# Six PSUM banks in turn, work given out ahead of read-outs, and wide tiles with their high weights first, in one layer of a hybrid decoder

## The chip, the cores and the metric

The kernel runs on one core of a Trainium2 chip. Its time is the device time of one execution in microseconds (us); lower is better. Names: PE is TensorE (PEld its weight loads), DVE is VectorE, ACT is ScalarE, POOL is GpSimd, SP is the queue that issues most DMAs.

## What is computed

One layer for a sequence of 256 positions and a width of 1024, in float32:

```
n = RMSNorm(x)
h = x + W_mix_out( g_conv * ConformerConv(n) + g_attn * DSA(n) )   # one input projection W_in of n
h = h + CrossAttn(RMSNorm(h), RMSNorm(mem))                        # 4 heads, 256 memory tokens
h = h + W2 relu(W1 RMSNorm(h))^2                                   # width 4096
out = RMSNorm(h)
```

ConformerConv gates a projection by a sigmoid, runs a causal depthwise convolution of 31 taps over the positions, takes a LayerNorm and a silu, and multiplies by a 1024 x 1024 matrix. DSA has 8 heads of 128, with a small index attention that chooses 64 keys for each query. All parameters are read once (92.21 MB from HBM with the inputs).

## The kernel before

**Activations stand feature by position**: a tile is 128 features x 256 positions, eight of them (`kt` 0 to 7) a tensor. Every float32 operand of a large product is split in two, a high part rounded to the matmul's format (`hi`) and the rest (`lo`), and a product is made of three: high weight by high activation, high by low, low by high. ACT makes `hi` of a weight by a copy and DVE makes `lo` by a subtraction, 1024 columns at a time; two such halves make a chunk of 1 MB that SP loads into one of three `raw` buffers. Up to six halves are held.

**The stream.** Chunks come in a fixed order, and so do the stages: xk (keys of the memory), conv (the convolution's input and gate, 4 of 8), qi and ki (index attention), conv (the other 4), gc (convolution gate), v, q and k in turn, ga (attention gate), ao (attention out), co (convolution out), mix (mix out), xq, xv and xo (cross attention), f1 and f2 in turn (feed forward; in the profile f and ff).

**A tile of 128 output features** is 8 steps `kt`. In a *narrow* tile (`mm3`) a step is three matmuls of 256 columns. In a *wide* one (`tile_b` with `wide`, L303) the high weight meets high and low activations side by side in one matmul of 512 columns, and the low weight the high activations in one of 256; the two halves of the PSUM bank are then added by `total` (L340): ACT copies the second half out, DVE adds the first. qi, q, k, ga, ao, xq and f are wide, conv, gc, co and mix narrow. Form b (`form_b`, L313) makes two such tiles of a chunk; each takes a PSUM bank from `ps_mm`, of which there are two. Four more banks (`ps_acc`) serve v, xv, xo, f2 and small products, two (`ps_aux`) the rest.

**What sets the order.** The program is written out by hand, engine by engine, with a running estimate of each engine's time (`Counted`: L89 is the line that issues every recorded instruction, so nearly all rows name it). After each tile `tick` (L247) resumes the `chains` (generators for heads, norms and the like), then gives DVE taps of the convolution from `fill` while its total is under PE's plus 1000 (ns), runs the read-outs' second halves that stand in `due`, and gives ACT one pair of tap products, which POOL adds into `added` by an accumulating DMA (42 of these). 148 taps are done on DVE (`acc`), the rest by those DMAs. ACT and DVE work off what they are given in that order.

**Around the middle.** When all taps are in, `layer_norm` normalises the convolution; it waits until the ga gate's sigmoid is done (`gates`), then takes silu on ACT and splits the result into `u2` on DVE (CAST and subtraction), which co needs. `gated` multiplies co's product by the gates, `residual` adds mix's product to `h_t` and splits it for xq. A cross head (`cross_head`) is a generator: scores, softmax, transposes, values.

Of the kernel before, what the change touches and what calls it, by code (L numbers as in the profile page):

```python
# [22 lines left out]
BEHIND = 1000  # L23
AHEAD = 1000
# [83 lines left out]
def block_kernel(ctx, tc, x, xt, mem, memt, wst, wki, vecs, convw, gout, out):  # L108
# [36 lines left out]

    class Pair:
# [99 lines left out]

    def tick():  # L247
# [4 lines left out]
        while later:  # L252
            later.pop(0)()
        if low_jobs and len(prepared) < READY and nturn[0] > 4:
            split_low()
        while (len(fill) > 1 or (fill and (len(done) > 5 or nused[0] < 5))) and dve.total < pe.total + (BEHIND if due else AHEAD):
            fill_one()
        while due:
            due.pop(0)()
        for g in groups:  # L260
            if g.ready() and scalar.total < pe.total + 1300:
                g.products()
                groups.remove(g)
                groups.append(g)
                break
        for g in halves:
            g.finish()
# [4 lines left out]
        dve.total = max(dve.total, pe.total - 2000)  # L272
        scalar.total = max(scalar.total, pe.total - 2000)
# [92 lines left out]
    def load_memory(q):  # L366
        for kt in ((0,), (2, 4), (6,), ())[q]:
            nc.sync.dma_start(mem_t[:, kt : kt + 2, :], memt[:, kt : kt + 2, :])

    load(4, load_memory)  # L370
# [21 lines left out]
    for j in range(9):  # L392
# [104 lines left out]
    def memory_parts():  # L497
# [4 lines left out]
        mem2.append(Pair("mem"))  # L502
        for kt in range(KT + 1):
            if kt < KT:
# [35 lines left out]
    class Half:  # L540
# [7 lines left out]
        def finish(self, now=False):  # L548
# [3 lines left out]
            self.open = False  # L552
            g = self.g
            both = acc[:, 4 * g : 4 * g + 4, :]
            dve.tensor_tensor(out=both, in0=both, in1=added[:, 4 * g : 4 * g + 4, :], op=ALU.add)
            pair = w2(f"usum{g}", F32, (P, 2, S))
# [162 lines left out]
    def layer_norm():  # L719
# [8 lines left out]
        for c, cs in enumerate(pairs):  # L728
# [3 lines left out]
            if c % 2 == 1:  # L732
                yield
# [524 lines left out]
```

## Time and profile before

| | us |
|---|---|
| median of 3 runs | 530.05 (529.81 to 530.83) |
| the profiled execution | 528.47 |
| its span, first to last instruction | 526.4 |
| PE busy / DVE / ACT / POOL | 507.4 / 400.9 / 322.3 / 44.6 |
| weights' lo on DVE, 161 | 195.2 |
| weights' hi on ACT, 161 | 168.1 |
| taps on DVE, 148 | 63.2 |

Where the stages lie, by the first matmul of each, in us from the span's start: conv 22.7, qi 45.9, ki 58.4, conv again to 90.2, gc 90.2, v 113.3, q and k 135.1, ga 190.7, ao 217.9, co 242.7, mix 268.2, xq 291.3, xv 305.3, xo 319.6, f 336.9. A row of a timeline gives start, length, engine, line, operation, what is written and read, the shape, how often in a row, and in brackets the engine's idle time before it and what ended it. Matmuls overlap their neighbours, so the pace of a stage is read from starts, not from lengths. A row of waits gives who waited for whom: us in total, times, longest.

### The profile page before, as it was taken

The page shows a single profiled execution, that of the slowest core. Times are in us where ns is not written, and L with a number is a line of the kernel's source. Part 1 is how long each engine was busy: PE and PEld are TensorE (multiplying, and loading weights), DVE is VectorE, ACT ScalarE, POOL GpSimd, SP SyncE. Part 2 cuts the span into 40 slices and gives each one's busy share as a digit, 9 for nine tenths or more (in the row PEclk, how much of TensorE's full clock was granted, in tenths as well). Part 3 has the DMA queues.
Part 4 walks back from the last instruction along what each step waited for, and adds up shares of the span by engine and source line. Part 5 has one row for each costly group of instructions (what it writes and reads, how often), then busy time and mean ns, then how long its engine had stood idle before and what let it go on. Part 6 is the DMA issues. An engine that isn't in the chain of part 4 may idle for free.

```text
span 526.4 us, 8078 instructions
## 1 busy us (share of the span) xinstructions
PE 507.4 (96%) x3081; PEld 449.5 (85%) x3081; DVE 400.9 (76%) x761; ACT 322.3 (61%) x579; POOL 44.6 (8%) x65
## 2 busy tenths in 40 slices
PE   7999999999899999998999999999999999999994
PEld 6998998998788888887999887978888888888883
DVE  2798999999996778878988875778666556665554
ACT  2765756776788898586457475565554545555422
POOL 0100221232322211000000000000000000000000
PEclk9999999999999999999999999999999999999999
DMA  8958875899999887464656434346555554555302
GB/s 276 350 189 243 246 212 166 235 248 262 287 281 260 212 199 220 131 220 166 217 202 227 178 133 159 131 156 235 170 220 176 217 177 159 200 199 196 125 1 80
DMA packets 21478, 104.79 MB, mean 199 GB/s; under 512 B 2496, under 2 KB 3392, under 8 KB 11072
## 3 DMA queue, kind: packets, MB, share of 16 engines
q1 hardware_dynamic: 14960, 92.90, 50.2%
q0 software_dynamic: 6048, 11.01, 12.1%
q8 instruction: 24, 0.39, 0.3%
q10 hardware_dynamic: 432, 0.36, 0.2%
q14 instruction: 14, 0.11, 0.1%
HBM read 92.21 MB, written 1.05 MB: 177 GB/s over the span
## 4 chain that ended last, share of the span: by engine, by line
PE 66%; DVE 16%; issue 5%; DMA 5%; ACT 5%; POOL 1%; SPq 0%; POOLq 0%; DVEq 0%; ACTq 0%
PE ps_ff L89 16%; PE ps_f L89 16%; DVE lo L89 6%; DVE acc L89 5%; PE ps_mix L89 4%; PE ps_k L89 4%; DMA raw<-in_wst_dram 4%; PE ps_co L89 4%; PE ps_ga L89 3%; PE ps_q L89 3%; PE ps_xo L89 3%; PE ps_xk L89 2%; PE ps_xq L89 2%; PE ps_xv L89 2%; DVE score L89 2%
## 5 line engine op out<-in xcount | busy, mean ns | idle before, releaser
L89 DVE TENSOR_TENSOR lo<-raw,hi 128x1024 fp32r<-128x1024 f32 (+1 forms) x161 | 195.2, 1216 | 2.6 <-ACT hi L89 2.6
L89 ACT ACTIVATE hi<-raw 128x1024 fp32r<-128x1024 f32 (+1 forms) x161 | 168.1, 1049 | 34.7 <-PE ps_ff L89 19.6
L89 PE MATMUL ps_f<-ff,hi 128*128 128x512 f32 x256 | 91.4, 399 | 1.3 <-DVE ft L89 1.3
L89 PE MATMUL ps_ff<-hi,fs 128*128 128x512 f32 (+1 forms) x264 | 82.6, 385 | 0.8 <-DVE h_rm L89 0.8
L89 PE MATMUL ps_f<-ff,lo 128*128 128x256 f32 x256 | 71.8, 281 | 0.0
L89 DVE SCALAR_TENSOR_TENSOR acc<-u,cw,acc 128x252 f32<-128x252 f32 (+18 forms) x148 | 63.2, 471 | 0.4
L89 PEld LDWEIGHTS ps_f<-ff,hi 128*128 128x128 f32 x256 | 48.1, 188 | 13.5 <-DVE ft L89 1.9
L89 PEld LDWEIGHTS ps_ff<-hi,fs 128*128 128x128 f32 x264 | 49.2, 188 | 11.1 <-DVE h_rm L89 1.0
L89 DVE TENSOR_TENSOR ft<-ps_f,ft 128x256 f32<-128x256 f32 x32 | 13.6, 425 | 55.8 <-ACT ft L89 55.6
L89 PE MATMUL ps_ff<-lo,fs 128*128 128x512 f32 (+1 forms) x132 | 50.7, 384 | 0.0
L89 PEld LDWEIGHTS ps_f<-ff,lo 128*128 128x128 f32 x256 | 48.4, 189 | 0.5
L89 PE MATMUL ps_conv<-n,hi 128*128 128x256 f32 x256 | 47.0, 286 | 1.4 <-DVE u L89 1.4
L536 POOL DMA_DIRECT2D added<-prod x42 | 36.5, 868 | 127.7 <-ACT prod L89 126.9
L89 PEld LDWEIGHTS ps_conv<-n,hi 128*128 128x128 f32 x256 | 39.8, 191 | 2.6 <-DVE u L89 1.8
L89 ACT ACTIVATE prod<-u,cw 128x226 f32<-128x226 f32 (+10 forms) x84 | 36.0, 478 | 1.3 <-DMA added<-prod 1.2
L89 PE MATMUL ps_conv<-n,lo 128*128 128x256 f32 x128 | 36.2, 283 | 0.0
L89 ACT ACTIVATE fs<-ft 128x256 fp32r<-128x256 f32 x32 | 13.4, 419 | 31.2 <-DVE ft L89 31.2
L89 PEld LDWEIGHTS ps_ff<-lo,fs 128*128 128x128 f32 x132 | 24.8, 188 | 4.3
L89 ACT ACTIVATE ft<-ps_f 128x256 f32<-128x256 f32 x32 | 12.2, 380 | 23.1 <-PE ps_f L89 21.6
L89 PE MATMUL ps_co<-u,hi 128*128 128x256 f32 x128 | 24.2, 287 | 1.4 <-DVE u L89 1.2
L89 PEld LDWEIGHTS ps_conv<-n,lo 128*128 128x128 f32 x128 | 24.5, 192 | 0.0
L89 PE MATMUL ps_k<-n,hi 128*128 128x512 f32 x64 | 23.1, 403 | 1.4 <-DVE q L89 1.4
(224 smaller groups left out, 1018.4 us busy)
## 6 DMA issues: line engine op xcount, KB each, us to landing
raw<-in_wst_dram SPq DMA_DIRECT2D x79, 1024.0 KB, 4.8
added<-prod POOLq DMA_DIRECT2D x42, 256.0 KB, 6.4
raw<-in_wst_dram SPq DMA_DIRECT2D x4, 512.0 KB, 8.3
mem_t<-in_memt_dram SPq DMA_DIRECT2D x4, 256.0 KB, 4.9
raw<-in_wst_dram SPq DMA_DIRECT2D x4, 256.0 KB, 6.0
x_rm<-in_x_dram SPq DMA_DIRECT2D x2, 512.0 KB, 7.5
mem_rm<-in_mem_dram SPq DMA_DIRECT2D x1, 1024.0 KB, 7.9
h_t<-in_xt_dram SPq DMA_DIRECT2D x1, 1024.0 KB, 6.8
```

The lines of the kernel that those rows point to most:

```text
L89: return fn(*args, **kwargs)
L536: nc.gpsimd.dma_start(added[:, ts, :].rearrange("p t n -> p (t n)"), prod[:, self.n, :, :].rearrange("p t n -> p (t n)"), accum_op=ALU.add)
```

## The change

- `tile_b`: a wide tile gives out its 8 matmuls with high weights first, then the 8 with low ones.
- gc, co and mix become wide, with the second half's read-out that this needs (`gate_conv`, `gated`, `residual`).
- `ps_turn`: tiles of form b take banks from mm and acc in turn (2 + 4), xq's second chunk from aux, the feed forward's from mm and aux.
- `meanwhile`, called behind a tile's matmuls and ahead of its read-outs: taps, up to two pairs of products, a weight's lo. `tick` keeps the read-outs' second halves and little else. AHEAD is 400 for 1000.
- Layer norm's silu precedes ga's sigmoid; the memory operand's split starts with ao (with up to 14 skipped turns) instead of mix; the products of `ya` and the gate and the scaling of `kx` move from co and mix to ao.
- Cross heads are written out between xq's tiles and xv's quarters; all four values follow xv.
- The first chunk and the memory come in halves instead of quarters, and one warming matmul fewer. xo's three products stand in another order (low weight before low activation). The last 512 columns are one piece of matmuls, read in two.

```diff
-BEHIND = 1000
-AHEAD = 1000
+AHEAD = 400
...
+    tags, turns = [("mm", 2), ("acc", 4)], [0]
+
+    def ps_turn(name):
+        turns[0] += 1
+        tag, bufs = tags[turns[0] % len(tags)]
+        return bank(tag, bufs, name)
...
+    def meanwhile():
+
+        if low_jobs and len(prepared) < READY and nturn[0] > 4:
+            split_low()
+        while later:
+            later.pop(0)()
+        for _ in range(2):
+            for g in groups:
+                if g.ready() and scalar.total + 800 < pe.total + AHEAD:
+                    g.products()
+                    groups.remove(g)
+                    groups.append(g)
+                    break
+        while may_fill() and dve.total < pe.total + AHEAD:
+            fill_one()
+        for g in halves:
+            g.finish()
...
-        while (len(fill) > 1 or (fill and (len(done) > 5 or nused[0] < 5))) and dve.total < pe.total + (BEHIND if due else AHEAD):
+        if due and may_fill() and dve.total < scalar.total:
             fill_one()
         while due:
             due.pop(0)()
-        for g in groups:
-            if g.ready() and scalar.total < pe.total + 1300:
-                g.products()
...
-        for kt in kts:
-            if wide:
+        if wide:
+            for kt in kts:
                 pe.matmul(ps, w[0][:, kt, :], x2.both(kt), start=kt == first, stop=False, skip_group_check=True)
+            for kt in kts:
                 pe.matmul(ps[:, :S], w[1][:, kt, :], x2.hi(kt), start=False, stop=kt == last, skip_group_check=True)
-            else:
+        else:
+            for kt in kts:
                 mm3(ps[:, :S], w[0][:, kt, :], w[1][:, kt, :], x2.hi(kt), x2.lo(kt), kt == first, kt == last)
...
-            ps = ps_mm(f"ps_{kind}{i}{ct}")
+            ps = ps_turn(f"ps_{kind}{i}{ct}")
             tile_b(ps, w, x2, wide=wide)
+            meanwhile()
             after(2 * i + ct, ps if wide else ps[:, :S])
...
-    load(4, load_memory)
+    load(2, load_memory)
...
+    def gate_conv(ct, ps):
+        total(gc_t[:, ct, :], ps)
+
+        def sigmoid():
+            act(gc_t[:, ct, :], gc_t[:, ct, :], AF.Sigmoid, bias=bgc[:, ct : ct + 1])
+
+        later.append(sigmoid)
...
-        while not gates:
+        while len(headed) < NH:
             yield
         act(table, table, AF.Silu)
...
     def gate_sigmoid():
-        while len(headed) < NH:
+        while not gates:
             yield
...
     def gated(ct, ps):
-        dve.tensor_tensor(out=gc_t[:, ct, :], in0=ps, in1=gc_t[:, ct, :], op=ALU.mult)
-        dve.tensor_tensor(out=gc_t[:, ct, :], in0=gc_t[:, ct, :], in1=ga_t[:, ct, :], op=ALU.add)
-        act(m2.hi(ct), gc_t[:, ct, :], AF.Copy)
+        t = w2(f"co{ct}", F32, (P, S))
+        total(t, ps)
...
+            dve.tensor_tensor(out=t, in0=t, in1=gc_t[:, ct, :], op=ALU.mult)
+            dve.tensor_tensor(out=gc_t[:, ct, :], in0=t, in1=ga_t[:, ct, :], op=ALU.add)
...
     def residual(x2, g):
         def go(ct, ps):
-            dve.tensor_tensor(out=h_t[:, ct, :], in0=ps, in1=h_t[:, ct, :], op=ALU.add)
-            act(x2.hi(ct), h_t[:, ct, :], AF.Copy, scale=g[:, ct : ct + 1])
+            dve.tensor_tensor(out=h_t[:, ct, :], in0=ps[:, :S], in1=h_t[:, ct, :], op=ALU.add)
             if low_due:
                 low_due.pop()()
+            dve.tensor_tensor(out=h_t[:, ct, :], in0=ps[:, S:], in1=h_t[:, ct, :], op=ALU.add)
+            scalar.after(dve.total + 100)
+            act(x2.hi(ct), h_t[:, ct, :], AF.Copy, scale=g[:, ct : ct + 1])
...
+        act(vx[:, 1, :S], accs[1][:, :S], AF.Copy, scale=rs_m[:, 1:2])
+        dve.tensor_scalar(vx[:, 1, S:], accs[1][:, S:], rs_m[:, 1:2], None, ALU.mult)
+        turned(3)
+        for h in range(XH):
+            value(h)
...
+    tags[:] = [("mm", 2), ("mm", 2), ("aux", 2), ("aux", 2)]
+    turns[0] = -1
     pending = [ff1(0), ff1(1)]
```

Three places in the order of instructions (a number behind a name tells buffers apart; x4 means four equal rows that follow each other). First TensorE at the first tile of gc, where `n` is the normalised input in two tensors of four `kt` each; before, with the end of conv ahead of it, and then the change, the whole tile:

```order
L89 MATMUL ps_conv_1068<-n_136,hi_1_831 128x256 x2
L89 MATMUL ps_conv_1068<-n_136,lo_1_832 128x256
L89 MATMUL ps_gc_1113<-n_135,hi_0_872 128x256 x2
L89 MATMUL ps_gc_1113<-n_135,lo_0_873 128x256
...
L89 MATMUL ps_gc_1113<-n_136,hi_0_872 128x256 x2
```

```order
L88 MATMUL ps_gc_1113<-n_130,hi_0_873 128x512 x4
L88 MATMUL ps_gc_1113<-n_131,hi_0_873 128x512 x4
L88 MATMUL ps_gc_1113<-n_130,lo_0_874 128x256 x4
L88 MATMUL ps_gc_1113<-n_131,lo_0_874 128x256 x4
L88 MATMUL ps_gc_1141<-n_130,hi_1_921 128x512 x4
```

The two rows of gc's first `kt` stand eight times over in the tile of before, once for each `kt`; now the low weight `lo_0` is first met behind eight matmuls of 512 columns.

Second DVE at the end of ao and the start of co: `ya` is the attention branch read out of ao's banks, `u_...` the split of the normalised convolution that co reads, `ga_t` and `gc_t` the gates. Before:

```order
L89 TENSOR_TENSOR ya<-ps_ao_2702,ya 128x256
L89 TENSOR_TENSOR lo_1_2667<-raw_2546,hi_1_2666 128x1024
L89 CAST u_2510<-acc 128x2x256
L89 TENSOR_TENSOR u_2510<-acc,u_2510 128x2x256
L89 TENSOR_TENSOR ya<-ps_ao_2733,ya 128x256
L89 TENSOR_TENSOR lo_0_2700<-raw_2607,hi_0_2699 128x1024
L89 CAST u_2510<-acc 128x2x256
L89 TENSOR_TENSOR u_2510<-acc,u_2510 128x2x256
L89 TENSOR_TENSOR ya<-ps_ao_2758,ya 128x256
L89 CAST u_2511<-acc 128x2x256
L89 TENSOR_TENSOR u_2511<-acc,u_2511 128x2x256
L89 CAST u_2511<-acc 128x2x256
```

and the change:

```order
L88 CAST u_2362<-acc 128x2x256
L88 TENSOR_TENSOR u_2362<-acc,u_2362 128x2x256
L88 TENSOR_TENSOR ga_t<-ya,ga_t 128x256 x2
L88 TENSOR_TENSOR ya<-ps_ao_2638,ya 128x256
L88 TENSOR_TENSOR lo_1_2636<-raw_2477,hi_1_2635 128x1024
L88 CAST u_2362<-acc 128x2x256
L88 TENSOR_TENSOR u_2362<-acc,u_2362 128x2x256
L88 TENSOR_TENSOR ga_t<-ya,ga_t 128x256 x2
L88 TENSOR_TENSOR ya<-ps_ao_2671,ya 128x256
L88 TENSOR_TENSOR lo_0_2669<-raw_2531,hi_0_2668 128x1024
L88 TENSOR_TENSOR ga_t<-ya,ga_t 128x256 x2
L88 TENSOR_TENSOR ya<-ps_ao_2698,ya 128x256
```

`ps_ao_2758` and `ps_ao_2725` (not shown) are the eighth tiles of ao; `ps_ao_2671` is the sixth. The last two casts of u stood behind the eighth add of ya and now stand ahead of the sixth, and products of ya and ga_t, which stood in co, follow them.

Third ACT in v, between the read-outs of its two halves (`prod` is a pair of tap products, each ending in one accumulating DMA). Before:

```order
L89 ACTIVATE v_rm<-ps_v_1431 128x512
L89 ACTIVATE prod<-u,cw 128x232 x2
L89 ACTIVATE hi_1_1535<-raw_1433 128x1024
L89 ACTIVATE prod<-u,cw 128x229 x2
L89 ACTIVATE hi_0_1558<-raw_1481 128x1024
L89 ACTIVATE prod<-u,cw 128x232 x2
L89 ACTIVATE hi_1_1583<-raw_1481 128x1024
L89 ACTIVATE prod<-u,cw 128x230 x2
L89 ACTIVATE hi_0_1606<-raw_1533 128x1024
L89 ACTIVATE v_rm<-ps_v_1530 128x512
```

and the change:

```order
L88 ACTIVATE v_rm<-ps_v_1376 128x512
L88 ACTIVATE hi_1_1480<-raw_1338 128x1024
L88 ACTIVATE prod<-u,cw 128x229 x2
L88 ACTIVATE hi_0_1505<-raw_1400 128x1024
L88 ACTIVATE prod<-u,cw 128x233 x2
L88 ACTIVATE prod<-u,cw 128x235 x2
L88 ACTIVATE hi_1_1531<-raw_1400 128x1024
L88 ACTIVATE prod<-u,cw 128x231 x2
L88 ACTIVATE hi_0_1556<-raw_1451 128x1024
L88 ACTIVATE prod<-u,cw 128x230 x2
L88 ACTIVATE v_rm<-ps_v_1477 128x512
```

Four pairs of products stood between the read-outs, and five do now. Of all 42, 8 stood ahead of gc's first read-out and 27 ahead of the second of k; now 12 and 34 do.

More of the change, by code (lines that the diff above doesn't have):

```diff
@@ L391, in block_kernel @@
     ps = ps_aux("ps_warm")
-    for j in range(9):
+    for j in range(8):
         nc.tensor.matmul(ps, zero_r[:, :P], zero_r, start=True, stop=True)
@@ L502, in memory_parts @@
         mem2.append(Pair("mem"))
+        skips = 14
         for kt in range(KT + 1):
+            while skips and dve.total > pe.total + 300:
+                skips -= 1
+                yield
             if kt < KT:
@@ L552, in finish, with add @@
             self.open = False
+            if now:
+                for _ in self.add():
+                    pass
+            else:
+                start(self.add())
+        def add(self):
             g = self.g
@@ L702, in form_a @@
                         kt == 0, kt == KT - 1)
+            meanwhile()
+            for rb in range(2):
                 if q == 3:
                     act(dst[:, rb, hf * 512 : hf * 512 + 512], accs[rb], AF.Copy, scale=scale[rb])
-            if q == 3 and ready is not None:
-                ready.append(True)
             tick()
+    while later:
+        later.pop(0)()
     act(table, table, AF.Exp)
@@ L766, in head @@
     def head(h, q, k):
+        yield
         yield
@@ L838, in block_kernel, with after_ao, branches @@
     ya = t8("ya")
+    memorised = start(memory_parts())
+    added_up = []
+    def after_ao(ct, ps):
+        total(ya[:, ct, :], ps)
+        due.append(lambda: added_up.append(ct))
+    def branches():
+        dve.tensor_tensor(out=kx, in0=kx, in1=mrb.unsqueeze(1).to_broadcast([P, XH, S]), op=ALU.mult)
+        while gating in chains:
+            yield
+        for ct in range(KT):
+            while ct >= len(added_up):
+                yield
+            dve.tensor_tensor(out=ga_t[:, ct, :], in0=ya[:, ct, :], in1=ga_t[:, ct, :], op=ALU.mult)
+            if ct % 2 == 1:
+                yield
     for i in range(4):
-        form_b("ao", i, o2, total_to(ya))
+        if i == 1:
+            branched = start(branches())
+        form_b("ao", i, o2, after_ao)
     while fill:
@@ L1013, in block_kernel, with after_xv, cross_values @@
-    form_a("xv", 0, mem2[0], vx, (rs_m[:, 0:1], rs_m[:, 1:2]), valued)
-    tick()
+        if ct == 2:
+            scores(0)
+            scores(1)
+        elif ct == 3:
+            soft(0)
+            soft(1)
+            scores(2)
+    def after_xv(q):
+        if q == 0:
+            turned(0)
+            soft(2)
+            scores(3)
+        elif q == 1:
+            turned(1)
+            soft(3)
+        elif q == 2:
+            turned(2)
+    def cross_values():
+        x2 = mem2[0]
+        accs = [ps_mm(f"ps_xv{rb}") for rb in range(2)]
+        for q in range(4):
+            wh, wl = weights("xv", q // 2, q % 2, 2)
+            split_ahead()
+            for rb in range(2):
+                rows = slice(rb * P, rb * P + P)
+                for k in range(2):
+                    kt = 2 * q + k
+                    mm3(accs[rb], x2.hi(kt)[:, rows], x2.lo(kt)[:, rows], wh[:, k, :], wl[:, k, :],
+                        kt == 0, kt == KT - 1)
+                if q == 3 and rb == 0:
+                    act(vx[:, 0, :], accs[0], AF.Copy, scale=rs_m[:, 0:1])
+            after_xv(q)
+            if q < 3:
+                tick()
+        act(vx[:, 1, :S], accs[1][:, :S], AF.Copy, scale=rs_m[:, 1:2])
[3 more added lines that the diff above has]
+            value(h)
+        tick()
@@ L1017, in block_kernel @@
+    sq_x.fold(True)
+    scaled = start(cross_scale())
+    form_b_late("xq", 0, c2, after_xq)
+    finish(scaled)
+    tags[:] = [("aux", 2)]
+    form_b("xq", 1, c2, after_xq)
+    finish(memorised)
+    cross_values()
     banks_of = {}
@@ L1052, in block_kernel @@
     form_c("xo", 0, dst, ox2, 0)
-    finish(heads[3])
     lows_of = []
```

155 lines of the change are left out of this document (72 added, 83 removed).

## The prediction

> **What bounds the kernel now.** First the page's busy time and, of its slices, the clock.
>
> ```profile
> span 526.4 us, 8078 instructions
> PE 507.4 (96%) x3081; PEld 449.5 (85%) x3081; DVE 400.9 (76%) x761; ACT 322.3 (61%) x579; POOL 44.6 (8%) x65
> PEclk9999999999999999999999999999999999999999
> ```
>
> TensorE is busy for 96% of the span at a full clock. A busy PE can still be a slowly issuing one, so I read the pace of matmuls next, from the chain in order of time and from the timeline of one feed-forward tile.
>
> ```profile
> 268.40 23.04 PE ps_mix L89 x192
> 374.60 5.64 PE ps_f L89 x32
> 380.24 5.46 PE ps_ff L89 x24
> ...
> 396.88 0.28 PE L89 MATMUL ps_f<-ff,lo 128*128 128x256 f32 x1
> 396.99 0.40 PE L89 MATMUL ps_f<-ff,hi 128*128 128x512 f32 x1
> 397.22 0.28 PE L89 MATMUL ps_f<-ff,lo 128*128 128x256 f32 x1
> 397.34 0.40 PE L89 MATMUL ps_f<-ff,hi 128*128 128x512 f32 x1
> ```
>
> In a run of 256-column matmuls one starts every 23.04 / 192 = 0.120 us; in a run of 512-column ones every 5.46 / 24 = 0.2275 us. The wide tile of before alternates the two and needs 5.64 / 16 = 0.3525 us a pair (397.34 - 396.99 = 0.35), against 0.2275 + 0.120 = 0.3475 for the two runs' paces. The rest of the span is what PE waits for; the list of waits, PE's rows:
>
> ```profile
> PE ps_k L89 <- DVE q L89: 1.4, 1, 1.4
> PE ps_conv L89 <- DVE u L89: 1.4, 2, 0.9
> PE ps_f L89 <- DVE ft L89: 1.3, 2, 1.0
> PE ps_co L89 <- DVE u L89: 1.2, 3, 0.5
> PE ps_xk L89 <- DMA raw<-in_wst_dram: 1.1, 1, 1.1
> PE ps_ao L89 <- DVE ya L89: 0.8, 1, 0.8
> PE ps_ff L89 <- DVE h_rm L89: 0.8, 1, 0.8
> PE ps_qi L89 <- DVE qi_t L89: 0.8, 1, 0.8
> PE ps_xo L89 <- ACT xptr L89: 0.7, 1, 0.7
> PE ps_xq L89 <- DVE qx L89: 0.6, 1, 0.6
> PE ps_xo L89 <- ACT kv L89: 0.3, 1, 0.3
> ```
>
> Six of these (q, conv's u, ft, ya, qi_t, qx; 8 waits, 6.3 us) have one form: a tile wants one of the two mm banks, and the tile two before it has not been read out. One (co) waits for its input. None waits for weights. A wait costs more than its row, as ends are modelled:
>
> ```profile
> 243.43 0.28 PE L89 MATMUL ps_co<-u,lo 128*128 128x256 f32 x1
> 244.20 0.38 PE L89 MATMUL ps_co<-u,hi 128*128 128x256 f32 x1 [0.49 <-DVE u L89]
> ...
> 246.64 0.69 DVE L89 TENSOR_TENSOR u<-acc,u 128x512 fp32r<-128x512 f32 x1
> ```
>
> The next start was due at 243.55 and came 0.65 later, not 0.49: about 0.16 more for each wait. So this is a kernel bound by PE's stream, with some 13 us of waits strewn over it.
>
> **The change, part by part.** *High weights first.* 72 wide tiles (4 qi, 8 each of q, k, ga and ao, 4 xq, 32 f) give out 8 matmuls of 512 and then 8 of 256. If each run keeps its own pace, a tile goes from 8 x 0.3525 = 2.82 to 8 x 0.3475 = 2.78 us: 72 x 0.04 = 2.9 us. Bounds: 0 if the pair's extra 0.005 us is not due to the order, and 2.9.
>
> *Three kinds made wide.* gc, co and mix have 24 tiles of 24 matmuls, 24 x 0.120 = 2.88 us each; they become 2.78: 24 x 0.10 = 2.4 us (1.4 us if a wide tile stays at 2.82). What this adds beside PE, at the rows of the same operations:
>
> ```profile
> L89 ACT ACTIVATE ya<-ps_ao 128x256 f32<-128x256 f32 x8 | 3.0, 370 | 2.3 <-PE ps_ao L89 2.3
> L89 DVE TENSOR_TENSOR ya<-ps_ao,ya 128x256 f32<-128x256 f32 x8 | 3.4, 420 | 3.1 <-ACT ya L89 3.1
> ```
>
> For each kind one more DVE add a tile (8 x 0.42 = 3.4 us) and for gc and co one more ACT read-out (8 x 0.37 = 3.0 us); mix takes its second half by a second DVE add, without ACT. That is 10.2 us of DVE and 6 us of ACT. They cost nothing while PE's 2.78 us a tile covers them; the cover is thin where DVE is full:
>
> ```profile
> 22.70:46.00 23.30, 23.30 (x195) 23.27 (x194) 21.68 (x36) 14.60 (x23) 1.05 (x1) 1.00 0.66 208
> 46.00:64.00 18.00, 17.25 (x114) 15.39 (x113) 16.60 (x37) 13.09 (x25) 2.83 (x4) 1.00 0.84 262
> 64.00:92.20 28.20, 26.80 (x222) 25.11 (x221) 27.39 (x72) 16.32 (x29) 5.76 (x8) 1.00 0.64 182
> 92.20:115.30 23.10, 23.10 (x186) 22.72 (x185) 22.83 (x54) 17.10 (x32) 6.80 (x9) 1.00 0.95 233
> 115.30:138.00 22.70, 22.70 (x106) 18.91 (x105) 22.70 (x45) 15.63 (x29) 6.88 (x8) 1.00 1.04 268
> 138.00:184.40 46.40, 44.96 (x270) 39.56 (x269) 37.66 (x93) 40.66 (x94) 12.04 (x14) 1.00 0.97 259
> 247.30:268.40 21.10, 21.01 (x175) 21.02 (x176) 19.67 (x37) 9.57 (x14) 0.00 (x0) 1.00 0.52 177
> 268.40:291.40 23.00, 23.00 (x193) 23.00 (x193) 19.67 (x32) 16.42 (x26) 0.00 (x0) 1.00 0.65 236
> ```
>
> (Columns: stretch, length, then busy PE, PEld, DVE, ACT, POOL, the clock, DMA share, GB/s.) In gc (92.2 to 115.3) and v (to 138) DVE has nothing free, so gc's 3.4 us push taps of the convolution later, into q and k, where 46.40 - 37.66 = 8.7 us are free. In co and mix DVE has 1.4 and 3.3 us free. co loses the 8 products of ya and ga_t (adds of the same shape: 3.4) to the ao stage and gains 3.4; mix gains 3.4 and loses kx's product and part of the memory operand. I take zero for all of it, with the lost third below as the price.
>
> *Six banks in turn, read-outs behind fill work.* Tiles alternate between 2 mm and 4 acc banks (xq: aux, f: mm and aux), so a tile waits for the read-out of the fourth tile before it or an older one: at least 5.5 us more leave. Every one of the 8 waits (longest 1.4 us) fits in that. Putting taps and products ahead of the read-out makes the read-out later by up to the planner's 400 ns plus one tap, which also fits. The most: 6.3 + 8 x 0.16 = 7.6 us.
>
> *co's input.* The silu of the convolution now precedes the ga sigmoid and the casts of u stand among ya's adds, the last of them ahead of ya's sixth add, not behind the eighth: two tiles (5.6 us) sooner. The most: 1.2 + 3 x 0.16 = 1.7 us.
>
> *Cross heads.* All four values follow xv's last tile, so the wait for the last xptr goes and that for kv stays: of 1.0 + 0.3 us about 0.7 can go.
>
> *Start and end.* Four loads of 512 KB replace eight of 256 KB ahead of the first tile; the same bytes go first through the same queue, so of the 1.1 us I take 0.4 (between -0.3 and 1.1). In the last block one 512-column piece replaces two of 256 in one bank: PE's 0.8 us wait goes, but two reads (0.42 us each by the row of ya) then follow the last matmul instead of one, and two products with them: 0.3, between -0.3 and 0.8.
>
> The waits come to 7.6 + 1.7 + 0.7 + 0.4 + 0.3 = 10.7 us. A faster PE meets the next-late thing, so I take two thirds, 7.1 us. **Sum** against the profiled execution's 528.47 us (span 526.4, 2.1 outside): -2.9 - 2.4 - 7.1 = -12.4, 516.1 us. The median of the runs shown stands 1.6 us over that execution, so 517.7; I say **517.5 us**.
>
> **The rivals.** *Every wait goes.* No wait of before is one for weights, and the new order lets low weights come 1.8 us later. 528.5 - 5.3 - 10.7 = 512.5, median 514.1. Against it: DVE and ACT gain work.
>
> *The order is worth nothing.* The pair's 5 ns would come from the mix of widths, or a run of 256 behind one of 512 pays it elsewhere. Then -1.4 - 7.1: 520.0, median 521.6. Runs of each width at their own pace speak against it. The Trainium skill, "TensorE: Matmul & The Clock Gate", section "Back-to-back issue gap", speaks for it: N/2.4 + 2.5 ns from start to start in a warm stream, whatever stands before, which as an estimate is 0.325 us for a pair in either order. The trace agrees neither with the figure (0.3525 alternating, 0.3475 by the two runs) nor, as far as these rows go, with the sameness.
>
> *The accumulating DMAs of the convolution.* From gc's first read-out to the second k, 20 tiles, ACT now gives out 22 pairs of products, each ending in one such DMA, where it gave 19. At that place they are already served one after another:
>
> ```profile
> 119.58 0.86 POOL L536 DMA_DIRECT2D added<-prod  x1 [2.36 <-ACT prod L89]
> 160.58 0.86 POOL L536 DMA_DIRECT2D added<-prod  x1 [1.81 <-ACT prod L89]
> DMA to landing us min/median/max: 3.6/6.4/11.2
> ```
>
> 14 intervals in 41.0 us are 2.93 us each, at a DMA share about 1.0. Three more take 8.8 us; a product must wait for its group's last landing, and behind it on ACT stand the halves hi of the weights and the read-outs. With the whole charged 517.5 + 8.8 = 526.3; half is covered by halves prepared ahead: 522. The Trainium skill, "DMA: Bandwidth & Descriptors", section "Queues, rings and completion order", has each DMA engine take turns between queues packet by packet; by that the weights keep their turn.
>
> *Slower: taps that lose their overlap.* On DVE the pitch of taps depends on their neighbours:
>
> ```profile
> 30.66 2.55 DVE L89 SCALAR_TENSOR_TENSOR acc<-u,cw,acc 128x254 f32<-128x254 f32 x5
> 131.41 1.62 DVE L89 SCALAR_TENSOR_TENSOR acc<-u,cw,acc 128x245 f32<-128x245 f32 x4
> L89 DVE SCALAR_TENSOR_TENSOR acc<-u,cw,acc 128x252 f32<-128x252 f32 (+18 forms) x148 | 63.2, 471 | 0.4
> ```
>
> Five of one channel tile in a chain take 0.51 us each; four that alternate, 0.385 (1.54 to the next instruction). If the new order chained all 148, DVE would need 148 x 0.125 = 18.5 and gc's 3.4 us more from 22.7 to 184.4, where 161.7 - 148.9 = 12.8 are free: 9.1 us over. No gain could be had in that stretch; outside it remain 1.6 (co, mix), 2.1 (52 tiles of ga, ao, xq and f) and 4.3 us (two thirds of the waits of f, ao, xq, co, xo, start and end): 530.05 + 9.1 - 8.0 = 531.2. It binds from a mean pitch of 0.45 and turns the sign at 0.50. Against it: the order of the taps still changes queue at each, and reads and lo stand between them.
>
> **How the numbers follow.** Forecast 0.48, every wait goes 0.22, accumulating DMAs 0.13, order worth nothing 0.10, slower 0.07. The range 512 to 525.5 leaves out the best part of the second case, the top of the DMA case and the slower one, under 2 in 10. About 1.06 us (0.2%) is what a measurement tells from no change. Faster 0.89, within it 0.04, slower 0.07.
>
> **What would show it.** Right: wide tiles of 2.78 us in ao and f, gc, co and mix at 22.2 us each, the rows q, u, ft, ya, qi_t gone from PE's waits, PE idle under 8 us. Wrong: a pair still at 0.352; PE rows that wait for hi or lo (DVE or ACT late with weights); ACT rows that wait for added in v and q; DVE taps near 0.5 us apart.

## The result, and the profile after

The changed kernel takes 524.41 us (median of 4 executions, 523.31 to 525.86), the kernel before, beside it, 529.93: a ratio of 0.9894 (95% interval 0.9867 to 0.9922), 5.5 us gained. The forecast was 517.5 us, 12.5 gained; the time lies inside the stated range, near its upper end. The profiled execution took 525.86 us, 2.6 less than the one of before. Medians and scatters here and below are over the executions that the ratios use, which leave out one slow execution each of one_ln2 (525.3), best2 (520.3), old_start and two_banks.

The page of the changed kernel, busy time and PE's clock in 40 slices:

```profile
span 524.1 us, 7696 instructions
PE 505.6 (96%) x2876; PEld 442.2 (84%) x2876; DVE 407.2 (78%) x786; ACT 327.2 (62%) x595; POOL 45.2 (9%) x65
PEclk9999999999988999999999999999999999999999
```

PE's share is as it was; the two 8s are new, and the mean clock fell from 0.998 to 0.992, which over 524 us is 3.1 us of full-speed work. Its list of waits, PE's rows (without the 1.9 us ahead of the first warm-up matmul, the same before and after), and one of ACT's:

```profile
PE ps_q L88 <- DVE q L88: 3.6, 1, 3.6
PE ps_s L88 <- DVE k L88: 2.3, 1, 2.3
PE ps_mrb L88 <- POOL rs_m L508: 1.6, 1, 1.6
PE ps_xk L88 <- DVE mem_t L88: 0.6, 1, 0.6
PE ps_mub L88 <- ACT ptr L88: 0.6, 1, 0.6
PE ps_o L88 <- ACT ptr L88: 0.4, 1, 0.4
PE ps_xq L88 <- DVE cx L88: 0.3, 1, 0.3
PE ps_f L88 <- DVE ff L88: 0.2, 1, 0.2
...
ACT prod L88 <- DMA added<-prod: 20.2, 14, 3.9
```

All eleven rows of before have gone (xk and xq now wait for other things). New ones stand in their place, and they sum to 9.6 us where the old ones were 10.4. Three are longer than any of before, and ACT now waits 20 us for landings of accumulating DMAs (1.2 before). The windows from 140 us on (columns as in the prediction) and the chain of waits there:

```profile
140.00:145.00 5.00, 5.00 (x30) 4.37 (x29) 5.00 (x11) 1.08 (x2) 0.86 (x1) 1.00 1.07 251
145.00:150.00 5.00, 1.42 (x8) 1.09 (x8) 1.44 (x3) 4.64 (x10) 1.72 (x2) 1.00 0.97 255
150.00:155.00 5.00, 3.49 (x14) 2.82 (x12) 3.89 (x10) 4.62 (x10) 2.49 (x3) 0.66 1.06 263
155.00:160.00 5.00, 4.22 (x15) 3.49 (x16) 5.00 (x10) 2.14 (x5) 0.96 (x2) 0.71 1.05 210
...
128.09 9.11 DMA added<-prod
...
140.15 10.86 DMA added<-prod
```

ACT and PE in order of time:

```profile
144.73 0.87 ACT L88 ACTIVATE prod<-u,cw 128x230 f32<-128x230 f32 x2 [3.92 <-DMA added<-prod]
145.50 1.06 ACT L88 ACTIVATE v_rm<-ps_v 128x512 f32<-128x512 f32 x2
...
148.17 0.37 ACT L88 ACTIVATE q<-ps_q 128x256 f32<-128x256 f32 x1
...
149.05 2.74 PE L88 MATMUL ps_q<-n,hi 128*128 128x512 f32 x8 [3.58 <-DVE q L88]
...
155.78 0.92 PE L88 MATMUL ps_s<-k,q 128*128 128x128 f32 x4 [2.29 <-DVE k L88]
156.35 3.29 PE L88 MATMUL ps_q<-n,hi 128*128 128x512 f32 x8
```

ACT stands for 3.92 us in front of a product whose group's last DMA has not landed; behind it, in its queue, are the read-outs of v and q; DVE's add of q follows them, and PE's next q tile that add. The bank it wants is that of the fourth tile before it, as the prediction said, but that tile's matmuls ended near 137 us and its add came at 148.57. Then, with the wait over, PE runs slowly: eight matmuls of 512 in 3.29 us (the eight of the k tile ahead of the wait took 2.00), at a granted clock of 0.66 and 0.71.

Where the gain stands is seen best when the span is cut at mix's first matmul, before (first row) and after (second):

```profile
268.24:526.40 258.16, 247.97 (x1382) 214.49 (x1380) 171.39 (x280) 137.32 (x224) 1.80 (x3) 1.00 0.47 167
```

```profile
271.09:524.10 253.01, 245.51 (x1306) 210.31 (x1304) 173.26 (x290) 137.25 (x225) 1.81 (x3) 1.00 0.46 165
```

From mix on, 5.15 us are won. Ahead of mix, 2.85 are lost: 1.07 of them before conv (23.75 against 22.68 us), and the most in q and k, as q starts 0.9 us sooner than before and ga, behind them, 6.1 later (196.76 against 190.65). The prediction's terms, put on the two sides of that cut, were 4.5 us behind it (mix 0.8, 36 wide tiles 1.4, two thirds of the waits of f, xq, xo and the end 2.3) and 7.9 ahead. So everything that failed lies ahead of mix.

### The profile page after: what moved, and what is told of

The parts are those of the page before. It is cut to its first block, busy times and chain, and to the rows that moved or that the text cites. A ratio compares the mean times of both kernels' runs of the same rounds, so it can differ in the third digit from the quotient of the medians.

```text
span 524.1 us, 7696 instructions
## 1 busy us (share of the span) xinstructions
PE 505.6 (96%) x2876; PEld 442.2 (84%) x2876; DVE 407.2 (78%) x786; ACT 327.2 (62%) x595; POOL 45.2 (9%) x65
## 3 DMA queue, kind: packets, MB, share of 16 engines
HBM read 92.21 MB, written 1.05 MB: 178 GB/s over the span
## 4 chain that ended last, share of the span: by engine, by line
PE 56%; DVE 22%; DMA 13%; ACT 5%; issue 3%; POOL 0%; POOLq 0%; DVEq 0%; ACTq 0%; SPq 0%
PE ps_f L88 17%; PE ps_ff L88 16%; DMA added<-prod 10%; DVE lo L88 8%; PE ps_ga L88 4%; DVE acc L88 3%; PE ps_xk L88 3%; PE ps_xo L88 2%; PE ps_k L88 2%; PE ps_xv L88 2%; DVE score L88 2%; PE ps_xq L88 2%; PE ps_ao L88 2%; DMA raw<-in_wst_dram 1%; DVE h_t L88 1%
## 5 line engine op out<-in xcount | busy, mean ns | idle before, releaser
L88 ACT ACTIVATE hi<-raw 128x1024 fp32r<-128x1024 f32 (+1 forms) x161 | 167.8, 1048 | 22.5 <-PE ps_ff L88 18.4
L88 PE MATMUL ps_ff<-hi,fs 128*128 128x512 f32 x256 | 81.7, 391 | 0.0
L88 PE MATMUL ps_f<-ff,hi 128*128 128x512 f32 x256 | 64.9, 393 | 0.2 <-DVE ff L88 0.2
L88 DVE SCALAR_TENSOR_TENSOR acc<-u,cw,acc 128x253 f32<-128x253 f32 (+18 forms) x148 | 62.2, 467 | 0.2
L88 PEld LDWEIGHTS ps_ff<-hi,fs 128*128 128x128 f32 x256 | 48.1, 188 | 9.7
L88 PEld LDWEIGHTS ps_f<-ff,hi 128*128 128x128 f32 x256 | 46.7, 188 | 9.8 <-DVE ff L88 1.1
L88 PE MATMUL ps_ff<-lo,fs 128*128 128x512 f32 x128 | 50.0, 390 | 0.0
L88 PEld LDWEIGHTS ps_f<-ff,lo 128*128 128x128 f32 x256 | 35.1, 190 | 2.5
L88 PE MATMUL ps_f<-ff,lo 128*128 128x256 f32 x256 | 36.0, 282 | 0.0
L88 ACT ACTIVATE ft<-ps_f 128x256 f32<-128x256 f32 x32 | 12.2, 380 | 22.5 <-PE ps_f L88 21.4
L88 PE MATMUL ps_q<-n,hi 128*128 128x512 f32 x64 | 18.4, 434 | 3.6 <-DVE q L88 3.6
L88 PE MATMUL ps_v<-hi,n 128*128 128x512 f32 x64 | 19.9, 389 | 0.0
```

Source lines behind the costliest of these rows:

```text
L88: return fn(*args, **kwargs)
```

## The experiments

Times are medians, ratios are to the kernel before on the same chip, with 95% intervals. Executions of one kernel scatter by 2 to 7 us, so steps under 2 us are read from the traces.

**The accumulating DMAs left out.** It shows what they cost in all. The convolution lacks 42 of its tap pairs; nothing else is changed.

```
-            nc.gpsimd.dma_start(added[...], prod[...], accum_op=ALU.add)
```

> The changed kernel (524.4 us) with the 42 accumulating DMAs left out: the products are still computed, but not added to the convolution. Theory (ACT waits for the accumulating DMAs, and the read-outs of v and q behind it come late): the rows PE ps_q <- DVE q (3.6 us) and PE ps_s <- DVE k (2.3) go, with them the lowered clock after them, and rs_m no longer stands behind an issue on POOL (1.6): 524.4 - 9.4 - 1.6 = about 513.5, between 512 and 516. Rival (DVE or ACT simply have too much elementwise work in v and q): both rows stay above 2 us, time 522 or more.

514.09 us (513.0 to 514.14), 0.9697 (0.9667 to 0.9727). PE's waits in it:

```profile
PE ps_xk L88 <- DVE mem_t L88: 0.6, 1, 0.6
PE ps_mub L88 <- ACT ptr L88: 0.6, 1, 0.6
PE ps_xq L88 <- DVE cx L88: 0.3, 1, 0.3
PE ps_f L88 <- DVE ff L88: 0.2, 1, 0.2
```

The waits for q, k and rs_m are gone though ACT still computes all 84 products and DVE does all the added work. So the added elementwise work by itself costs nothing, as the prediction had it, and 10.3 us hang on the DMAs. (The kernel before was not run without its DMAs, so how much of this it pays too is not known.) The DMA share from 140 to 145 us fell with them:

```profile
140.00:145.00 5.00, 5.00 (x31) 4.41 (x30) 5.00 (x11) 3.37 (x9) 0.00 (x0) 1.00 0.50 144
```

**Is it their number at this place, or that they stand ahead of the read-outs?** In one kernel a tile gives out one pair of products at most; in the other they stand behind the read-outs, by the old rule.

```
-        for _ in range(2):          # one_product
+        for _ in range(1):
             for g in groups: ...
```

> The changed kernel with at most one pair of products to a tile instead of two (8 instead of 10 in v, 1 instead of 2 behind the second q; the total stays 42). Theory A (it is the number of products: more per time than the DMAs can land): the waits for q and k go or shrink below 1 us each, 515 to 518. Theory B (it is their place: they stand ahead of the read-outs on ACT, and any wait for a landing delays these): most of the loss stays, 521 to 524.5. Rival (elementwise work): no change, 524.4.

> The changed kernel with the products given out behind the read-outs, one to a tick at most, by the rule of the kernel before; all else as changed. Theories A and B both: waits for q and k below 1 us each, 515 to 518; if one_product stays near 524 and this comes near 516, the place decides. Rival (elementwise work): no change, 524.4.

one_product 522.98 us, 0.9874 (0.9828 to 0.9921); behind 523.86, 0.9869 (0.9824 to 0.9914). Both have lost the wait for q and nearly all of that for k (0.5 and 0.8 us left), so the mechanism was right. Neither gained more than 1.5 us: one_product has the waits of theory A and the time of theory B, and behind misses its 515 to 518. How long k waits is not settled by one profile, though: other kernels with one product to a tile have 2.3 (one_ln2), 2.7 (one_ln3) and 1.0 us (best2). With two, q and k together wait 4.5 to 6.6 us in six profiles (the changed kernel, alternate, ln3, warm12, old_start, stand), with one 0.5 to 2.7 in four. PE of one_product, in order of time:

```profile
239.22 0.63 PE L88 MATMUL ps_co<-u,hi 128*128 128x512 f32 x2
241.41 0.73 PE L88 MATMUL ps_co<-u,hi 128*128 128x512 f32 x2 [1.57 <-DVE u L88]
242.48 0.73 PE L88 MATMUL ps_co<-u,hi 128*128 128x512 f32 x2 [0.33 <-DVE u L88]
245.98 1.22 PE L88 MATMUL ps_co<-u,hi 128*128 128x512 f32 x2 [2.77 <-DVE u L88]
```

PE reaches co 9.5 us sooner than in the changed kernel (239.2 against 248.75) and stands there for the convolution's result, 4.7 us in three waits; from 244 to 251 us its clock is at 0.51, and mix starts only 1.8 us sooner. DVE shows why it is late, the sum of the convolution and the last subtraction that makes u, of the kernel before first and then of the changed one:

```profile
213.33 1.22 DVE L89 TENSOR_TENSOR acc<-acc,added 128x1024 f32<-128x1024 f32 x1
```

```profile
205.95 1.23 DVE L88 TENSOR_TENSOR acc<-acc,added 128x1024 f32<-128x1024 f32 x1
...
247.52 0.69 DVE L88 TENSOR_TENSOR u<-acc,u 128x512 fp32r<-128x512 f32 x1
```

Before, the last u started at 246.64, 33.3 us behind the sum. Now the sum comes 7.4 us sooner and u 41.6 us behind it, no sooner than before. The change had put one more `yield` behind the sum (`add`) and one more ahead of the norm's first matmul (`layer_norm`), each a tick: 2.8 us in ao, 2.9 to 5.0 in ga, where the heads' matmuls come between. The whole difference lies there: from the sum to that matmul (`ps_mub`, at 217.70 and 218.91) it is 4.4 us before and 13.0 now, from there to the end of the last u 29.6 and 29.3.

**The layer norm given out sooner.** Two or three of those ticks are taken out, with one product to a tile (one_ln2, one_ln3) or two as in the change (ln3).

```
         u2.append(Pair("u2"))
-        yield
-        yield                        # one_ln2: one of these
         mub = ps_aux("ps_mub")[:, :S]
 ...
-        yield
         yield
         rs = rsqrt(vs[:, 0, :], "vr")
```

> one_product (522.98 us, where the loss had gone from q and k to three waits of co for u, 4.7 us, and a lowered clock behind them) with the layer norm behind the convolution given out two ticks (5.6 us) sooner. Theory C (the convolution with its accumulating DMAs ends late whatever the spacing; what q no longer pays co pays, as the chain from the last DMA to u is as long as before): co's waits fall from 4.7 to under 0.5 us and the clock there stays full: 7 us less, 515 to 517. Rival (PE waits at co for something else that is late, the adds of ya or the gate): co's waits stay above 3 us, 522 or more.

> The same with three ticks (8.4 us) sooner. Theory C: the same as with two, 515 to 517 (nothing waits for u any more; what goes beyond is not on the path). If the layer norm's own steps on DVE are what is late, ps_mub or ps_vr now wait for it, by 1 to 3 us, and it comes out at 517 to 520.

> The changed kernel with the layer norm given out three ticks sooner and nothing else (two products to a tile as in the change). If the two losses stand one behind the other (TensorE comes to co at 248.8 us because of q and k, when u is just there): nothing is won where q and k stall as in the changed kernel's profile, 522 to 524.5, with the last u some 8 us ahead of co. If the norm alone holds the kernel up: 516 to 518 as in one_ln3.

one_ln2 517.43 us, 0.9768 (0.9683 to 0.9854); one_ln3 516.63, 0.9747 (0.9713 to 0.9781); ln3 522.35, 0.9863 (0.9788 to 0.9937). co's waits for u are down to 0.8 us in one_ln2 and gone in one_ln3. As a square:

| us | norm as changed | three ticks sooner |
|---|---|---|
| two products to a tile | 524.4 | 522.4 |
| one product | 523.0 | 516.6 |

From the timelines, us: the sum of the convolution, the end of the last u, the first matmul of co and of mix, the span.

| | sum | last u | co | mix | span |
|---|---|---|---|---|---|
| before | 213.3 | 247.3 | 242.7 | 268.2 | 526.4 |
| changed | 205.9 | 248.2 | 248.7 | 271.1 | 524.1 |
| one_product | 204.8 | 245.9 | 239.2 | 269.3 | 521.7 |
| ln3 | 202.5 | 235.6 | 244.4 | 266.8 | 519.5 |
| one_ln3 | 205.2 | 239.3 | 239.9 | 262.2 | 515.2 |
| no_accum | 194.2 | 236.5 | 237.0 | 259.3 | 512.2 |

Either cure alone gave 1.4 to 2.1 us, which is not clear of the scatter; both gave 7.8, which is. In the changed kernel two things stand one behind the other: PE comes to co at 248.7 because of q and k, and u is there at 248.2. Take away one, and the other holds. ln3 shows the half that one_product can't: u ready 8.8 us ahead of co, and no more gained. From the sum to the end of the last u it is 41.2 to 42.3 us in the six profiles that have the change's norm, banks and places (the changed kernel, alternate, warm12, old_start, no_accum, one_product), and 33.1 and 34.1 in ln3 and one_ln3.

**What the banks, and the places of taps and products, are worth.** Six banks alone in the kernel before; the changed kernel on two banks; the changed kernel with taps and products behind the read-outs (in this one the gate's sigmoid comes ahead of the second half's add, so the gate is not the reference's; the operations are the same).

```
-            ps = ps_mm(f"ps_{kind}{i}{ct}")      # before_banks
+            ps = ps_turn(f"ps_{kind}{i}{ct}")

-    tags, turns = [("mm", 2), ("acc", 4)], [0]   # two_banks
+    tags, turns = [("mm", 2)], [0]
 ...                                              # and so in xq and the feed forward
```

> The kernel before with one part of the change alone: its tiles take mm and acc banks in turn (mm and aux in the feed-forward tiles) instead of the two mm banks; order of matmuls, narrow tiles, places of products and taps all as before. By the prediction's term the 8 waits for read-outs go and 7.6 us with them: 522.4. If more banks alone uncover the next-late thing (the landings of the accumulating DMAs), some of it comes back as waits for q, k or u: 524 to 528.

> The changed kernel with its wide tiles and conv tiles on the two mm banks again, all else as changed (524.4 us). By the prediction's term the waits for read-outs come back: 7 to 8 us more, 531 to 532, with rows PE ps_k <- DVE q, ps_f <- DVE ft, ps_ao <- DVE ya. By what before_banks showed (a bank only lets TensorE run on to the first matmul that reads the late tile): 524 to 527, in gc to q no more than now, with rows for f, qi and conv of 1 us each at most.

> The changed kernel with taps and products given out behind a tile's read-out on ACT again, and products by the rule before; banks, order of matmuls and all else as changed. If placing them ahead of the read-outs is what makes q and k late: the waits at q and k fall under 1 us and co pays as in one_product and behind, 521 to 524. If the place is worth what it was made for: waits for u, qi_t, q of 1 us each come on top, 526 or more.

before_banks 530.87 us, 1.0016 (0.9988 to 1.0044): nothing. two_banks 534.04, 1.0100 (1.0026 to 1.0175): by the ratios (1.0100 - 0.9894, of 530) 11 us more than the changed kernel, with some 4 us of uncertainty, and more than either expectation said. Its longest waits:

```profile
PE ps_k L88 <- DVE q L88: 4.7, 1, 4.7
PE ps_qi L88 <- DVE qi_t L88: 2.3, 1, 2.3
```

read_first 527.36, 0.9945 (0.9916 to 0.9975): 2.9 more. It has no wait for q and 1.2 us for k, and pays 6.3 us at co, as its convolution's sum comes at 215.6. PE's waits in before_banks, and what ACT does ahead of the late one:

```profile
PE ps_s L89 <- DVE k L89: 3.7, 1, 3.7
...
PE ps_ff L89 <- DVE ft L89: 1.6, 1, 1.6
PE ps_co L89 <- DVE u L89: 1.6, 3, 0.9
...
138.69 1.06 ACT L89 ACTIVATE hi<-raw 128x1024 fp32r<-128x1024 f32 x1 [1.02 <-DMA raw<-in_wst_dram]
...
146.56 0.37 ACT L89 ACTIVATE k<-ps_k 128x256 f32<-128x256 f32 x1
```

The waits for q (as a bank), u and qi_t are gone, but the first head needs k itself, and k is no earlier: ACT works from 138.69 to 146.9 with 0.17 us of idle time and comes to this tile 5 us after PE is done with it. The wait of 1.4 us for a bank became one of 3.7 for the data, with a slow clock behind it (0.58 from 148 to 152 us). In the feed forward it became a wait of ff for ft. Up to gc the banks had paid in this profile: conv started 1.05 us later than before, gc 1.9 sooner (88.30 against 90.20). In the changed kernel, where taps and products stand ahead of the read-outs, the same banks are worth 11 us; that a tile's bank is held longer there is the likely reason, and was not measured. So here this part paid only beside the others; which of them most (the places, the wide tiles) was not tried apart. One of these others is a further `yield` that the change puts at the start of `head`: it gives out a head's first product, which reads k, a tile later. before_banks does not have it, and six banks with this yield alone were not run.

**The order in the wide tiles undone**, high and low weights in turn:

> The changed kernel with high and low weights in turn again in the wide tiles (512, 256, 512, 256 ...). By the prediction's term (0.04 us a tile, now 96 wide tiles): 96 x 0.04 = 3.8 us more, about 528. By the rival (order worth nothing): 524.4 within 1 us, with pairs of 0.3475 us in the timeline or the same tile time of 2.78 us.

525.98 us, 0.9922 (0.9899 to 0.9945): 1.6 above the changed kernel's median, which with this scatter can't be told from 3.8 nor surely from nothing. The trace can: the chain of waits has, for mix's eight tiles and two of f, here

```profile
271.65 22.61 PE ps_mix L88 x128
...
373.55 5.65 PE ps_f L88 x32
```

and with the new order, in one_product's chain for mix and in the changed kernel's for f,

```profile
269.44 22.39 PE ps_mix L88 x128
```

```profile
384.99 5.56 PE ps_f L88 x32
```

so 0.028 us a tile for mix and 0.045 for f (0.040 by the starts of ten later pairs of tiles, 5.64 against 5.56). If all 96 tiles did so, the order would be worth about 96 x 0.035 = 3.4 us of PE's stream, an estimate. Not all do: the first six tiles of f take 17.62 us with the new order and 17.06 in turn, so that all 32 tiles of f together gain 0.44 us. Why those six are slower stays open.

**The start.** Twelve warm-up matmuls instead of eight; or the old loads and nine.

> The changed kernel with 12 warm-up matmuls instead of 8 (the last ends near 7.5 us instead of 5.7). Start theory 1 (the ten or so xk matmuls that start 0.52 us apart instead of 0.22 are slow because TensorE had stood still for 0.6 us just before): their pace comes back, conv starts 1.5 to 2 us sooner (3 us won, 1.2 lost to the longer warm-up), 522.5 to 523. Start theory 2 (they are slow because their inputs come late or for another reason): conv starts 1.2 us later or at the same place, 524.4 to 525.6.

> The changed kernel with the kernel before's start (eight loads of 256 KB ahead of the first tile, nine warm-up matmuls). The traces have conv start at 23.75 us in the changed kernel and at 22.68 before: if the loads and the warm-up are the whole reason, conv starts at 22.7 and the time is 1.1 us less, 523.3. If the new start is worth something behind it (x_rm is there 0.9 us sooner), 524.4 or more.

warm12 523.10 us, 0.9869 (0.9841 to 0.9898); old_start 524.45, 0.9899 (0.9866 to 0.9933). conv starts at 22.69 and 23.53 us. But one_product, with the changed start untouched, has it at 22.72, and no_accum at 23.78. The start moves by a microsecond from execution to execution whatever it is made of, so neither theory is borne out as it stands. The traces show two ways to be late. In the changed kernel, no_accum, behind and ln3 (conv at 23.6 to 23.8) the first eight of xk's matmuls start 0.43 us apart, which is the pace at half clock (below), and come to 0.22 at about 10 us; in all the others they start 0.22 us apart from the second on. old_start and before_banks (23.5 and 23.7) run at full pace but wait 2.0 and 2.2 us for a chunk. In the rest conv starts at 22.5 to 22.7. What decides between the clocks at the start no run shows.

**TensorE made to stand still.** At four quiet places of the feed forward a spare matmul waits for 2, 6, 10 and 20 memsets on POOL.

```
+    def stand(c, n):
+        j = w2(f"stall{c}")
+        act(j, g_out[:, :512], AF.Copy)
+        for k in range(n):
+            nc.gpsimd.memset(j, 0.0)
+        ps = ps_aux(f"ps_stall{c}")
+        pe.matmul(ps, j[:, :P], j, start=True, stop=True)
 ...
+        if c in (2, 5, 8, 11):
+            stand(c, {2: 2, 5: 6, 8: 10, 11: 20}[c])
```

> The changed kernel with TensorE made to stand still at four quiet places of the feed-forward stage (a matmul of a spare tile that waits for 2, 6, 10 and 20 memsets of it on POOL; nothing else reads it). If a long stand lowers the granted clock behind it, the matmuls of 512 columns after the longer stands start 0.3 us or more apart instead of 0.23 for some microseconds, and after the shortest one not, and the clock of the windows behind falls below 0.9: price of a stand of 4 us about 6. If the low clock behind q's stall has another cause (the load of DMAs there), all four show full pace at once behind the stand.

It ran once (551.5 us). PE, in order of time: each stand and the eight matmuls of 512 behind it.

```profile
370.92 1.13 PE L88 MATMUL ps_stall<-stall 128*128 128x512 f32 x2 [2.37 <-POOL stall L1283]
371.48 2.41 PE L88 MATMUL ps_f<-ff,hi 128*128 128x512 f32 x8
...
407.66 1.84 PE L88 MATMUL ps_stall<-stall 128*128 128x512 f32 x2 [2.50 <-POOL stall L1283]
408.50 3.75 PE L88 MATMUL ps_f<-ff,hi 128*128 128x512 f32 x8
...
448.33 2.07 PE L88 MATMUL ps_stall<-stall 128*128 128x512 f32 x2 [4.83 <-POOL stall L1283]
449.42 3.77 PE L88 MATMUL ps_f<-ff,hi 128*128 128x512 f32 x8
...
495.10 2.08 PE L88 MATMUL ps_stall<-stall 128*128 128x512 f32 x2 [10.65 <-POOL stall L1283]
496.19 4.23 PE L88 MATMUL ps_f<-ff,hi 128*128 128x512 f32 x8
```

Behind the stand of 2.37 us the matmuls run at full pace from the second on, behind those of 2.50, 4.83 and 10.65 us at half pace (by their single starts 0.427 us apart instead of 0.228) until 3.7 to 5.0 us behind the stand. From the start of the spare matmuls to that of the first matmul behind the eight it is 2.81, 4.43, 4.69 and 5.16 us: against the shortest, 1.6, 1.9 and 2.35 us more. The price hardly depends on the length of the stand: a wait of 2.5 us costs 4.1, one of 4.8 costs 6.7.

**The account closed.** Accumulating DMAs matched to the pace at which they land (five ticks between a group's products, 34 of them, the rest as taps on DVE), a variant with them spread evenly, and both good forms with the spread of rs_m two tiles later. All four stand on one_ln3.

```
-ADDED = (11, 11, 10, 10)                              # s5_10_7 and best
+ADDED = (10, 10, 7, 7)
-    ... nturn[0] >= self.issued + 3
+    ... nturn[0] >= self.issued + 5
         nc.gpsimd.tensor_tensor(out=rs_m, ...)
         yield
+        yield                                         # best, best2
+        yield
```

> one_ln3 (516.6 us) with the accumulating DMAs matched to the pace at which they land: a group's next product after five ticks instead of three (six instead of eight products in v), and 34 instead of 42 of them in all (the other 8 become 16 more taps on DVE, 0.42 us each, 7 us). Theory A with C (backlog of DMAs at q and k, and the end of the convolution at co): the wait of k (2.3 to 2.7 us) and the lowered clock behind it go, co does not wait: 4 to 5 us less, 511.5 to 513. If DVE's taps are now what ends last, co or q wait for DVE: 516 or more.

> The same with four ticks and the 34 products spread evenly (9, 9, 8, 8): eight products in v as in one_ln3, so by theory A the wait of k stays at 1 to 2.5 us, and only the end is relieved: 514 to 516.5. If it comes out like s5_10_7 it was the total, not the pace in v.

> s5_10_7 (518.0 us; its profile shows one wait left that the kernel without accumulating DMAs has not, 2.4 us for rs_m at 55 us, with a lowered clock behind it) with the spread of rs_m given out two tiles later. If the account of the loss is whole: 3 to 4 us less, 514 to 515, and PE's waits are those of no_accum. If another late thing takes its place: 516 or more.

> one_ln3 (516.6 us; all 42 accumulating DMAs, 2.7 us wait for k) with the spread of rs_m two tiles later: where rs_m came in time in one_ln3's profile nothing changes, where it did not 1 to 3 us go: 515 to 516.5, the wait of k stays at 1 to 3 us. By the account, best is 1 to 2 us below it.

s5_10_7 518.01 us, 0.9780 (0.9756 to 0.9804); s4_f8_ln3 520.71, 0.9835 (0.9772 to 0.9898); best 515.73, 0.9721 (0.9685 to 0.9758); best2 514.77 (512.48 to 518.63), 0.9718 (0.9654 to 0.9782). s5_10_7 lost the wait for k as expected, and met another: rs_m, 2.38 us, with a clock of 0.58 for 4 us behind it. POOL's power for it stood behind a DMA issue (at 54.51 us, the power from 55.08, for 1.57 us instead of 0.70 in no_accum). With its spread moved, no wait for it is left: best comes to 1.6 us above no_accum. best2, with all 42 DMAs, can't be told from best, against what was expected; that their number no longer matters is not shown by this, as best2 scatters by 6 us. s4_f8_ln3 was a miss: k does not wait in its profile though v has as many products as one_ln3, and co waits 3.5 us, since the sum ends later (210.6). That the taps which DVE took over are the reason is not shown: s5_10_7 has as many, and its two sums lie between 206.3 and 208.6. best is 8.7 us under the changed kernel's median and 14.3 under the kernel before. PE's longest waits in it:

```profile
PE ps_s L88 <- DVE k L88: 1.9, 1, 1.9
PE ps_xk L88 <- DVE mem_t L88: 1.2, 2, 0.7
PE ps_pt L88 <- ACT att_p L88: 0.6, 1, 0.6
```

The wait for k is not wholly gone, so pacing the DMAs was not all of it; at 1.9 us it leaves the clock at 1.00 in this profile.

## Why the prediction was right and wrong

*What bounds the kernel.* Right in kind: PE's stream with waits strewn over it. Wrong in one thing: the waits were summed as if each stood for itself.

*High weights first, and three kinds made wide.* Right in mechanism and, tile by tile, in size. Tiles of mix and f come to 2.80 and 2.78 us, and undoing the order alone gives the pair's 0.352 back. In sum it is less, as f's first six tiles lose part of it. The formula without a term for the order (the Trainium skill, "TensorE: Matmul & The Clock Gate", section "Back-to-back issue gap") does not hold for these matmuls: by it, as an estimate, a matmul of 512 takes 0.216 us, one of 256 takes 0.109 and the pair 0.325, where the trace has 0.2275 and 0.120 by runs and 0.353 (5.65 / 16) in turn.

*Added elementwise work at zero.* Right: no_accum has all of it, and no wait from it.

*Six banks in turn: "Every one of the 8 waits fits in that."* This is the step that failed first. The rows named a bank, but what they showed was a late read-out, and the read-out has a second customer, whoever reads the data: the first head for k, ff for ft. before_banks gained nothing of the 7.6 us in all; what it won up to gc went into the wait for k and the clock behind it. The prediction asked how long a bank may be held, not when the data is needed.

*co's input: "two tiles (5.6 us) sooner."* This is the step that failed second, and it cost as much: with one product to a tile, the norm's ticks are worth 6.4 us (523.0 to 516.6), and with those ticks out, the second product 5.7 (522.4 to 516.6). u's last part came at 248.2 us, not sooner than 247.3. The order of the casts was read rightly, but the two new `yield`s between the sum and the norm's first matmul lengthened the way from the sum to u from 34.0 to 42.3 us (last u's end less the sum's start), which ate the 7.4 us by which the sum came sooner. And co was costed as one wait of 1.7 us, where it is a gate: whatever is won ahead of co is lost there unless u moves as far. 7.9 of the 12.4 us were forecast ahead of mix; in their place 2.85 were lost.

*The accumulating DMAs* (chance 0.13; 522, at most 526.3). This rival is the one that happened, in its place and by its sign, ACT rows that wait for added in v and q. Its working was only half right. It charged three more products in that stretch; with one product to a tile (one_product) 523.0 us remained. The DMAs cost 10.3 us in all because they also set when the sum is done, and because a wait behind them is long enough to lower the clock, which no term of the prediction had. What queue takes which turn no run here shows.

*Every wait goes* (514.1). It was out of reach for the change as made, but not far off for the kernel: 514.1 without the DMAs (whose taps are then missing from the result), and with them 515.7 (best) and 514.8 (best2). *The order is worth nothing* and *taps that lose their overlap*: neither happened (DVE's 148 taps 62.2 us in the page after, 63.2 before).

*Start and end.* The start moves by a microsecond between executions, so the 0.4 us could not be seen. The end's wait went. "None waits for weights" was a misreading of the list: xk's row, 1.1 us for `raw`, does.

## What to carry to other kernels

A wait for a bank is a late read-out: before giving it more banks, ask who reads the data next, and when; here more banks paid only together with what makes the read-out late on purpose. Where a side chain joins the main stream (here the convolution at co), cut the profile there and cost each side by itself: gains ahead of the joint count only as far as the side chain moves too, so count the ticks on it. When two late things stand one behind the other, curing either looks worthless; only the square of both tells.

## What was not expected of the hardware

In the middle of a stream, waits of TensorE of 2.1 to 10.7 us were, with one exception, followed by matmuls 0.427 us apart instead of 0.228, which cost 1.6 to 2.35 us beyond the wait itself in the run with stands. The length of the wait alone does not decide it: the clock fell behind 2.10 us in ln3, 2.12 in alternate and 2.27 in one_ln2 and not behind 2.37 in stand, and it fell behind three waits of together 1.6 us at co in before_banks (0.76 from 245 to 250 us), the longest of them 0.9.

The traces' record of the clock shows why. The clock stands at 1 or at a half, a half lasts 3.41 us or a whole multiple (3.41, 6.83 and 13.65 in stand), and so do the full stretches between two halves (34.1 us, twice, in stand): it is set in steps of 3.41 us. I cut all 19 traces at these steps, from 20 us to the last matmul, and counted in each step at full clock the time that its matmuls fill at full pace (0.23 us for 512 columns, 0.125 for 256, 0.07 for fewer). All 24 steps filled to 0.38 or less were followed by one at half clock; none of those filled to 0.42 or more was. The wait of 2.37 us lay across two steps (1.84 us in the first, which was filled to 0.42), that of 2.10 in ln3 within one. A step at half clock holds 1.7 us less work.

The Trainium skill, "TensorE: Matmul & The Clock Gate", section "Part 1: The HAM clock gate", has half the clock after an idle window of about 3.4 us. The half and the length of the window agree with the trace; that the window be idle does not, as one filled to 0.38 was enough.

The executions of the changed kernel and its variants with accumulating DMAs scatter by 2.3 to 7.3 us here; those of no_accum lie within 1.1. The DMAs alone do not explain it, as the four executions of the kernel before beside the changed one, with 42 of them, lie within 1.1 too (13 beside later runs within 4.7).
